# Full-height operands for the small products of a streaming encoder step: zero-padded planes for the remainder of k, and 128 rows and columns for the sample's products and transposes

## The chip, the cores and the metric

One core of one Trainium2 chip runs the whole kernel in one launch. The time is device microseconds of one execution, and the kernel before is given as the median of 3 runs. The trace shows one more, profiled execution. TensorE is called PE, its weight loads PEld, VectorE DVE, ScalarE ACT, GpSimd POOL and the queue that issues the DMAs SP.

## The reference, cut to what matters

The function is one step of a one-layer encoder on two inputs at once: a prompt of 512 rows and a sample of 32 rows with a cache of 512 earlier positions. D is 1024, and everything is f32.

```
h = rms_norm(x);  q, k, v, xb, gb, qc = split(h @ w_in)
# A: differential attention, 8 heads, two 64-wide q/k maps a head, 128-wide values
logits[m] = q_m . k_m / 8 + bias      (m = 0, 1; masked by blocks of 64 positions)
w = softmax(logits[0]) - lam * softmax(logits[1]);  a = rms_norm(w @ v)
# B: a gated linear recurrence over a width-4 convolution of xb
# C: cross attention of qc (4 heads x 256) into 256 memory rows
x += (gate_a * a@Wa + gate_b * b@Wb + gate_c * c@Wc) @ w_out
x += (silu(g) * u) @ w_ffn_out;       y = rms_norm(x)
```

The sample does the same with the cached keys and values in front of its own 32, and with its own cached memory rows. Keys, values, recurrent states and the memory's keys and values are outputs too.

## The kernel before, in words

Activations lie transposed, with features on the 128 partitions and the 544 = 512 + 32 positions in the free dimension. Every large product is made from split operands: an f32 value is held as a high part rounded to fp32r and a low part, the remainder, and a product is high·high + high·low + low·high, each a one-pass fp32r matmul. `gemm` (line 413) does this per 128 output features in two halves of 272 columns into one of two accumulators in PSUM (`acc`). Four further PSUM banks (`side`) serve everything small. Weights come in 1 MB chunks and are split by ACT (`wh`) and DVE (`wl`).

The order of instructions on each engine is fixed when the kernel is built. The class `Flow` (line 48) plays main generators and helper generators against each other by estimated costs: a helper that says `yield t` goes on when the planner's clock reaches t, and `fl.take`/`fl.give` hand out buffers. `MM` (line 307) charges a matmul by its columns alone, whatever its row count. On the chip each engine then runs its list in that order and waits on semaphores.

Stages: the memory's products and the input norm; then "attn" (pairs p = 0..3 of heads, lines 1101 to 1109): the q, k and v products of two heads on the main line, with everything else of the pair slipped in between; then "lru"; then "cross"; then the output product and the FFN. What the change touches:

- `k_evac` (line 869) makes of each head's k a tile `ka` [128, 2, 512]: per map m, the 64 rows of that map's high part in their own half and again in the other half. The remainder goes to `kl` [128, 512], each map in its own 64 rows. `qa` [128, 2, 544] has, per map, the high part of q in the map's rows and the remainder in the others.
- `unit` (line 980), 32 of them, one per head and block of 128 queries, makes the logits of two maps. Per map it issues two products over N = 256, 256, 384 or 512 keys: one over 128 rows (`ka`, which gives high·high + low·high) and one over the map's 64 rows (`kl`, high·low). DVE then adds the bias and takes the minimum (line 1000), ACT makes the exponential, DVE merges the maps, PE transposes (`ident,e`), ACT or DVE copies, and PE multiplies with v (`vn,wt`).
- `natural` (line 856) transposes v: four 128×128 blocks and the sample's 32 columns.
- `sample` (line 916), 4 of them: the sample's attention over 544 keys for two heads. Weights `es` [128, 544] are combined by products with `cm` (four blocks of 128 columns and one of 32), copied to `wts`, and multiplied with the cached v (`vc`) and the new v (`vn`, 32 rows).
- `cross_sample` (line 1391), 4 of them: the sample's cross attention, with 32 columns of q as stationary operand, and a transpose of [32, 256].
- `row_norm` (line 534): sums of squares per position by products with a column of ones, in blocks of 128 positions and a last one of 32, a reciprocal root on DVE, and products with the identity that spread it over the partitions.
- `MB` (line 788): parts of the later tile `m`, lent to the attention stage. `mb done` is the event after which `gate_a` (line 1114) may write the first gates into `m`.

Of the kernel before, what the change touches and what calls it, by code (L numbers as in the profile page):

```python
# [9 lines left out]
F32 = mybir.dt.float32  # L10
# [179 lines left out]
def hybrid_step(ctx: ExitStack, tc, io):  # L190
# [29 lines left out]
    def slot_tile(pool, shape, dt, tag):  # L220
        return pool.tile(shape, dt, name=tag, tag=tag, bufs=NB[tag])
# [312 lines left out]
    def row_norm(pool, sqs, n, rb, ev, late=None):  # L534


        blocks = [(i, min(P, n - i * P)) for i in range((n + P - 1) // P)]
        full = n // P
        v = tu(pool, [P, len(blocks)], F32, "rs")
        if full < len(blocks):  # L540
            nc.vector.memset(v[:, full:], 1.0)

        banks = len(blocks) if len(sqs) > 1 else 1
        yield from fl.take(*["side"] * banks)
        pss = [side_tile() for _ in range(banks)]
        for a, sq in enumerate(sqs):
            if a:
                yield from fl.get(late)
            for i, r in blocks:
                MM(pss[i % banks][:r, i:i + 1], sq[:, i * P:i * P + r], ones_d, a == 0, a == len(sqs) - 1)  # L550
        yield fl.now + 100
        for i, r in blocks if banks > 1 else [(slice(0, full), P)] + blocks[full:]:
            ps = pss[i % banks if banks > 1 else 0]
            cols = i if isinstance(i, slice) else slice(i, i + 1)
            t = VS(v[:r, cols], ps[:r, cols], EPS, None, OP.add)
# [8 lines left out]
        for i, r in blocks:  # L564
            o = (i % 4) * P
            MM(pss[i // 4][:, o:o + r], y[:r, i:i + 1].to_broadcast([r, P]), ident[:r, :r], True, True)
        if rb is None:
            S[ev, "bank"] = pss[0]
            fl.set(ev, fl.now + 100)
            return  # L570
        yield fl.now + 100
        for q in range(nb):
            m_ = min(512, n - q * 512)
            t = COPY(rb[:, q * 512:q * 512 + m_], pss[q][:, :m_])
            fl.give("side", t)
        fl.set(ev, t)
# [210 lines left out]

    MB = {"kcT": (0, 1024), "bs": (2048, T), "qpad": (2048 + 2 * T, 256)}

# [66 lines left out]
    def natural(src, dst, j):  # L856
        yield from fl.take("side", "side")
        ps, p2 = side_tile(), side_tile()
        for t in range(4):
            TR(ps[:, t * P:(t + 1) * P], src[:, t * P:(t + 1) * P])  # L860
        TR(p2[:TS, :P], src[:, TP:])
        yield fl.now + 100
        t1 = COPY(dst[:, 0:4, j * P:(j + 1) * P], ps.rearrange("p (t d) -> p t d", t=4))
        t2 = VC(dst[:TS, 4, j * P:(j + 1) * P], p2[:TS, :P])
        fl.give("side", t1)
        fl.give("side", t2)
        yield max(t1, t2)

    def k_evac(at, p, j):
        def go(acc):  # L870
            yield from fl.take("t1")
            kf = t1_tile()
            t = COPY(b2(kf), acc[:, :, :HT])
            give_acc(t)
            S["kf", p, j] = kf
            yield t
# [8 lines left out]
            S["k", p, j] = (ka, kl)  # L885
            yield t
            for m_ in range(2):
                r = slice(m_ * 64, m_ * 64 + 64)
                t = LO(kl[r], kf[r, :TP], ka[r, m_])
            fl.set(("k", p, j), t)  # L890
            for i in range(4):
                fl.spawn(member("attn", unit(at, p, j, i)))
        return lambda acc: member("attn", go(acc))

    def v_evac(at, p, j):
        def go(acc):
# [4 lines left out]
            if j == 0:  # L901
                yield from fl.take("vn")
                S["vn", p] = slot_tile(at, [P, 5, 256], F32, "vn")
            yield t
# [11 lines left out]
    def sample(at, p):  # L916
# [18 lines left out]
        fl.give("bs", t)  # L935
        if p == 3:
            fl.set("mb done", t)
        yield t + 100
# [7 lines left out]
        ps = side_tile()  # L946
        wts_ = slot_tile(at, [P, 5, 64], F32, "wts")
# [6 lines left out]
        t = VC(wts_[:TS, 4], ps[:TS, 256:320])  # L954
        fl.give("side", t)
# [3 lines left out]
        for j in range(2):  # L959
            for t in range(5):  # L960
                r = P if t < 4 else TS
# [18 lines left out]
    def unit(at, p, j, i):  # L980
# [9 lines left out]
        for m_ in range(2):  # L990
            r = slice(m_ * 64, m_ * 64 + 64)
# [18 lines left out]
        if S["units", p, j] == 4:  # L1010
            for tg in ("qa", "ka", "kl"):
                fl.give(tg)
            fl.give("b4", t)
        yield t + 100
# [39 lines left out]
    def finalize(at, p):  # L1054
        if S["left", p]:
            return
        fl.give("vn")
        mn, sm, ss, cc = S["st", p]
        r0 = tu(at, [P, 8], F32, "r0")
# [331 lines left out]
    def cross_sample(cr, h):  # L1391
# [7 lines left out]
        yield from fl.take("ce", "side")  # L1399
        sx = side_tile()[:TS, :NMEM]  # L1400
        for j in range(2):
            MM(sx, S["qsm"][:, 2 * h + j], ckT[:, j], j == 0, j == 1)
        fl.give("ck")
        e = slot_tile(cr, [P, NMEM], F32, "ce")[:TS]
        yield fl.now + 100
# [6 lines left out]
        pts = tu(cr, [P, 2, TS], F32, "pts")  # L1412
        yield fl.now + 100
        t = VC(pts, ps[:, :2 * TS].rearrange("p (t q) -> p t q", t=2))
        fl.give("side", t)
# [6 lines left out]
        fl.give("cv")  # L1422
        yield fl.now + 100
        pov = po[:, :2 * TS].rearrange("p (n q) -> p n q", n=2)
# [214 lines left out]
    def main():  # L1639
# [23 lines left out]
        with tc.tile_pool(name="attn", bufs=1, reuse_waits="tile") as at:  # L1663
            declare(kcT=2, vc=1, bs=2, b4=3, qpad=2, qa=2, ka=2, kl=2, vn=2, es=1, cm=1,
                    wts=1, e=4, wt=2, on=2, ajunk=1)
# [24 lines left out]
        with tc.tile_pool(name="cross", bufs=1, reuse_waits="tile") as cr:  # L1690
            S["cr"] = cr
            declare(mraw=2, mh=2, ml=2, cq=4, ce=4, pth=1, ptl=1, ck=1, cv=1)
            S["qsm"] = tl(cr, [P, 8, TS], F32, "qsm")
            ch = tl(actp, [P, KD, T], F32R, "ah")
# [102 lines left out]
```

## Time and profile before

| what | value |
|---|---|
| median of 3 runs (lowest, highest) | 1266.03 us (1261.21, 1267.73) |
| profiled execution, device time | 1265.88 us |
| its span | 1264.0 us |
| mean granted clock of TensorE | 0.990 |
| PE busy, PEld busy | 1249.7 us (99%), 1214.8 us (96%) |
| DVE, ACT, POOL busy | 677.3 us (54%), 466.7 us (37%), 28.6 us (2%) |

Busy time of PE counts each matmul from its start to its modelled end, and neighbours overlap. So how fast PE goes is read from the starts of its matmuls in the timeline, not from its busy share. A shape such as 64\*128 64x256 is rows × columns of the stationary operand and then rows × columns of the moving one. An f32 product that isn't fp32r appears as two records.

### The profile page before, as it was taken

Reading aid. Unit: us, or ns where it says so; the run is one execution under the profiler, and the core shown is the slowest. Engines: PE = TensorE matmul, PEld = TensorE weight load, DVE = VectorE, ACT = ScalarE, POOL = GpSimd, SP = SyncE. Lnnn points to the kernel's source line nnn. Section 1 sums busy time; section 2 is a strip of 40 time slices with the busy share of each in tenths; the row PEclk is TensorE's granted clock in tenths of the full one; section 3 lists DMA queues with packets and bytes.
Section 4 is the critical chain, followed back from the end, with each engine's and each line's share of the span. In section 5 each row is a group of like instructions: output and inputs, shape, how many; then the busy total and the mean of one; then the engine's idle time right before and its main releaser. Section 6 shows DMA issues by size and latency. Waiting matters only on the chain.

```text
span 1264.0 us, 22469 instructions
## 1 busy us (share of the span) xinstructions
PE 1249.7 (99%) x9620; PEld 1214.8 (96%) x9620; DVE 677.3 (54%) x1338; ACT 466.7 (37%) x781; POOL 28.6 (2%) x88
## 2 busy tenths in 40 slices
PE   8999999999999999999999999999999999999996
PEld 8998989898999999999999999999999999999996
DVE  6875767676526787644545334554344343344235
ACT  6635343434325556732323322343222231222122
POOL 0002000000000111000000000000000000000001
PEclk9999899999999999999999999999999999999998
DMA  7772323231131322233143233222221222212212
GB/s 265 243 239 86 132 85 132 86 102 52 67 109 68 109 76 90 87 118 121 64 139 100 102 132 101 76 92 77 91 101 68 101 79 89 101 68 101 85 51 71
DMA packets 36835, 131.19 MB, mean 104 GB/s; under 512 B 4184, under 2 KB 15832, under 8 KB 25088
## 3 DMA queue, kind: packets, MB, share of 16 engines
q1 hardware_dynamic: 36736, 129.76, 30.2%
q8 instruction: 75, 1.23, 0.4%
q14 instruction: 24, 0.20, 0.0%
HBM read 118.81 MB, written 13.68 MB: 105 GB/s over the span
## 4 chain that ended last, share of the span: by engine, by line
PE 96%; DVE 2%; DMA 1%; ACT 0%; issue 0%; SPq 0%; DVEq 0%; ACTq 0%
PE acc L308 84%; PE side L308 10%; PE side L315 2%; DMA mk_d<-mkf 1%; DMA raw<-in_w_mem_kv 0%; DVE wl L249 0%; DVE x L258 0%; DVE xT L258 0%; DVE rst L249 0%; DVE al L249 0%; ACT wh L236 0%; DVE m L249 0%; ACT m L236 0%; SPq L300 0%; DVE hl L249 0%
## 5 line engine op out<-in xcount | busy, mean ns | idle before, releaser
L308 PE MATMUL acc<-hh,wh 128*128 128x272 f32 x1856 | 389.7, 291 | 0.0
L308 PE MATMUL acc<-hl,wh 128*128 128x272 f32 x1856 | 388.0, 290 | 0.0
L236 ACT ACTIVATE wh<-raw 128x1024 fp32r<-128x1024 f32 (+1 forms) x179 | 187.6, 1049 | 356.5 <-PE acc L308 333.6
L308 PEld LDWEIGHTS acc<-hh,wh 128*128 128x128 f32 x1856 | 292.5, 189 | 2.0 <-issue 0.9
L308 PEld LDWEIGHTS acc<-hl,wh 128*128 128x128 f32 x1856 | 292.0, 189 | 0.4 <-issue 0.2
L249 DVE TENSOR_TENSOR wl<-raw,wh 128x1024 fp32r<-128x1024 f32 (+1 forms) x180 | 217.2, 1208 | 103.8 <-PE acc L308 78.9
L308 PE MATMUL acc<-hh,wl 128*128 128x272 f32 x1856 | 258.3, 289 | 0.0
L308 PEld LDWEIGHTS acc<-hh,wl 128*128 128x128 f32 x1856 | 241.9, 189 | 1.2 <-issue 0.6
L249 DVE TENSOR_TENSOR t<-acc,rb 128x544 f32<-128x544 f32 x44 | 31.9, 725 | 151.3 <-PE acc L308 151.2
L308 PE MATMUL acc<-ah,wh 128*128 128x272 f32 (+2 forms) x480 | 101.4, 288 | 0.0
L308 PE MATMUL acc<-al,wh 128*128 128x272 f32 (+2 forms) x480 | 101.3, 289 | 0.0
L308 PE MATMUL acc<-bl,wh 128*128 128x272 f32 x384 | 79.6, 288 | 0.0
L308 PE MATMUL acc<-bh,wh 128*128 128x272 f32 x384 | 79.5, 288 | 0.0
L249 DVE TENSOR_TENSOR x<-acc,x 128x544 f32<-128x544 f32 (+2 forms) x35 | 23.6, 675 | 103.2 <-PE acc L308 103.2
L308 PEld LDWEIGHTS acc<-ah,wh 128*128 128x128 f32 x480 | 76.4, 188 | 0.0
L308 PEld LDWEIGHTS acc<-al,wh 128*128 128x128 f32 x480 | 76.2, 188 | 0.0
L308 PE MATMUL acc<-ah,wl 128*128 128x272 f32 (+2 forms) x480 | 66.0, 288 | 0.0
L308 PEld LDWEIGHTS acc<-ah,wl 128*128 128x128 f32 x480 | 62.4, 188 | 0.0
L308 PEld LDWEIGHTS acc<-bh,wh 128*128 128x128 f32 x384 | 60.4, 188 | 0.0
L308 PEld LDWEIGHTS acc<-bl,wh 128*128 128x128 f32 x384 | 60.1, 188 | 0.0
L308 PE MATMUL acc<-bh,wl 128*128 128x272 f32 x384 | 52.8, 289 | 0.0
L308 PEld LDWEIGHTS acc<-bh,wl 128*128 128x128 f32 x384 | 49.8, 188 | 0.0
(248 smaller groups left out, 1325.9 us busy)
## 6 DMA issues: line engine op xcount, KB each, us to landing
raw<-in_w_in SPq DMA_DIRECT2D x24, 1024.0 KB, 4.9
raw<-in_w_ffn_in SPq DMA_DIRECT2D x22, 1024.0 KB, 4.9
raw<-in_w_gate SPq DMA_DIRECT2D x12, 1024.0 KB, 5.0
raw<-in_w_ffn_out SPq DMA_DIRECT2D x8, 1024.0 KB, 4.9
raw<-in_w_mem_kv SPq DMA_DIRECT2D x7, 1024.0 KB, 5.7
raw<-in_w_proj_a SPq DMA_DIRECT2D x4, 1024.0 KB, 5.0
raw<-in_w_proj_b SPq DMA_DIRECT2D x4, 1024.0 KB, 4.9
raw<-in_w_proj_c SPq DMA_DIRECT2D x4, 1024.0 KB, 4.9
```

Source lines behind the costliest of these rows:

```text
L236: nc.scalar.activation(out, in_, func, scale=scale, bias=bias, accum_out=accum_out)
L249: nc.vector.tensor_tensor(out, a, b, o)
L308: nc.tensor.matmul(out, lhsT=lhsT, rhs=rhs, start=start, stop=stop)
L315: nc.tensor.transpose(out, in_, ident[:n, :n])
```

## The change

Products over fewer than 128 rows or onto fewer than 128 columns get operands of 128.

- The remainder of k becomes [128, 2, 512] per head, one plane per map, with the other map's 64 rows zero. Two such tiles are made and zeroed once when the attention stage opens, and handed round by a list. The `kl` product then runs over all 128 rows.
- The sample's part of `vn` and `wts` gets zero rows below the 32 (zeroed once), and the products run over 128 rows.
- The last block of `es`, of v, and of the squares is the last 128 positions rather than the last 32, and the results are read from rows 96 to 127.
- The sample's queries of the cross attention are the last 128 columns, in a tile with two buffers, and its softmax and transposes run over 128 rows. The softmax's small statistics are columns of one tile.
- `es` moves into the lent part of `m`, so `mb done` comes after the products that read it.

```diff
@@ row_norm
-        blocks = [(i, min(P, n - i * P)) for i in range((n + P - 1) // P)]
+        blocks = [(i, min(i * P, n - P)) for i in range((n + P - 1) // P)]
-            for i, r in blocks:
-                MM(pss[i % banks][:r, i:i + 1], sq[:, i * P:i * P + r], ones_d, a == 0, a == len(sqs) - 1)
+            for i, o in blocks:
+                MM(pss[i % banks][:, i:i + 1], sq[:, o:o + P], ones_d, a == 0, a == len(sqs) - 1)
-            MM(pss[i // 4][:, o:o + r], y[:r, i:i + 1].to_broadcast([r, P]), ident[:r, :r], True, True)
+            c, r = (i % 4) * P, min(P, n - i * P)
+            MM(pss[i // 4][:, c:c + r], y[:, i:i + 1].to_broadcast([P, P]), ident[:, P - r:], True, True)
@@ natural
-        TR(p2[:TS, :P], src[:, TP:])
+        TR(p2[:, :P], src[:, T - P:])
@@ k_evac
-            kl = slot_tile(at, [P, TP], F32R, "kl")
+            i_kl = S["kl free"].pop(0)
+            kl = S["kl", i_kl]
-                t = LO(kl[r], kf[r, :TP], ka[r, m_])
+                t = LO(kl[r, m_], kf[r, :TP], ka[r, m_])
@@ unit
-            MM(s_[:, :N], qa[r, m_, i * P:(i + 1) * P], kl[r, :N], False, True)
+            MM(s_[:, :N], qa[:, m_, i * P:(i + 1) * P], kl[:, m_, :N], False, True)
@@ sample
-        es = slot_tile(at, [P, T], F32, "es")
+        es = mb("es", 0)
-        if p == 3:
-            fl.set("mb done", t)
...
-        MM(ps[:TS, 256:320], es[:, PAST:], cm, True, True)
+        MM(ps[:, 256:320], es[:, T - P:], cm, True, True)
         fl.give("es")
+        if p == 3:
+            fl.set("mb done")
...
-                lw = vc[:, t, j * P:(j + 1) * P] if t < 4 else vn[:TS, 4, j * P:(j + 1) * P]
-                MM(ps[:, j * TS:(j + 1) * TS], lw, wts_[:r, t, j * TS:(j + 1) * TS], t == 0, t == 4)
+                lw = vc[:, t, j * P:(j + 1) * P] if t < 4 else vn[:, 4, j * P:(j + 1) * P]
+                MM(ps[:, j * TS:(j + 1) * TS], lw, wts_[:, t, j * TS:(j + 1) * TS], t == 0, t == 4)
@@ soft_rows
-        st = tu(S["cr"], [P, 3], F32, "cst")[:s_.shape[0]]
+        i_st = S["cst n"] = S.get("cst n", -1) + 1
+        st = S["cst"][:, 3 * i_st:3 * i_st + 3]
@@ c_evac
+            if j == 0:
+                yield from fl.take("qs")
+                S["qs", h] = slot_tile(cr, [P, 2, P], F32, "qs")
+                fl.set(("qs", h))
+            yield from fl.get(("qs", h))
-            t = VC(S["qsm"][:, 2 * h + j], acc[:, 1, HT - TS:HT])
+            t = VC(S["qs", h][:, j], acc[:, 1, HT - P:HT])
@@ cross_sample
-            MM(sx, S["qsm"][:, 2 * h + j], ckT[:, j], j == 0, j == 1)
+            MM(sx, S["qs", h][:, j], ckT[:, j], j == 0, j == 1)
-            TR(ps[:, t * TS:(t + 1) * TS], e[:, t * P:(t + 1) * P])
+            TR(ps[:, t * P:(t + 1) * P], e[:, t * P:(t + 1) * P])
@@ main, where the attention stage opens
+            S["wts"] = tl(at, [P, 5, 64], F32, "wts")
+            S["vn free"] = [tu(at, [P, 5, 256], F32, "vnz") for _ in range(2)]
+            for z in [S["wts"]] + S["vn free"]:
+                nc.vector.memset(z[:, 4], 0.0)
+            S["kl free"] = [0, 1]
+            for q in S["kl free"]:
+                S["kl", q] = tu(at, [P, 2, TP], F32R, "klz")
+                for m_ in range(2):
+                    nc.vector.memset(f(S["kl", q][64 - m_ * 64:128 - m_ * 64, m_]), 0.0)
```

## Rows read from the trace of the kernel before

**Rows 1.** Busy time by stage: us, busy and count by engine, clock, DMA.
```profile
core 0: us, PE busy (x) PEld busy (x) DVE busy (x) ACT busy (x) POOL busy (x), PEclk, DMA share, GB/s
80.00:346.00 266.00, 266.00 (x1845) 238.59 (x1844) 178.90 (x554) 106.44 (x255) 7.96 (x24) 0.98 0.31 104
346.00:540.00 194.00, 194.00 (x1546) 194.00 (x1546) 128.52 (x178) 107.56 (x169) 15.53 (x54) 1.00 0.26 88
```
**Rows 2.** The page's chain that ended last, by engine.
```profile
PE 96%; DVE 2%; DMA 1%; ACT 0%; issue 0%; SPq 0%; DVEq 0%; ACTq 0%
```
**Rows 3.** Waits of the weight loads in the attention stage: total us, times, longest.
```profile
PEld side L308 <- issue: 11.0, 51, 0.3
...
PEld side L308 <- DVE on L265: 0.2, 1, 0.2
...
PEld side L308 <- DVE e L258: 0.2, 1, 0.2
```
**Rows 4.** Timeline of PE, logits of 256, 384 and 512 keys: start, us.
```profile
86.69 0.28 PE L308 MATMUL side<-ka,qa 128*128 128x256 f32 x1
86.90 0.38 PE L308 MATMUL side<-kl,qa 64*128 64x256 f32 x1
87.21 0.38 PE L308 MATMUL side<-ka,qa 128*128 128x256 f32 x1
...
89.09 0.52 PE L308 MATMUL acc<-hh,wl 128*128 128x272 f32 x2
...
118.33 0.42 PE L308 MATMUL side<-ka,qa 128*128 128x384 f32 x1
...
119.79 0.55 PE L308 MATMUL side<-cm,es 128*128 128x64 f32 x3
...
123.11 0.40 PE L308 MATMUL side<-ka,qa 128*128 128x512 f32 x1
...
124.72 0.41 PE L308 MATMUL side<-wts,vc 128*128 128x32 f32 x2
```
**Rows 5.** Timeline of PE, 128-row products in the cross attention's logits.
```profile
563.22 0.40 PE L308 MATMUL side<-mh,cq 128*128 128x256 f32 x2
...
565.00 0.42 PE L308 MATMUL acc<-bl,wh 128*128 128x272 f32 x2
```
**Rows 6.** Groups by form on PE: count, busy, mean ns.
```profile
L308 PE MATMUL side<-kl,qa 64*128 64x256 f32 x32 | 12.2, 381 | 0.0
L308 PE MATMUL side<-kl,qa 64*128 64x512 f32 x16 | 7.9, 495 | 0.0
L308 PE MATMUL side<-kl,qa 64*128 64x384 f32 x16 | 7.0, 438 | 0.0
```
**Rows 7.** Timeline of PE, the sample's small products.
```profile
107.75 0.71 PE L315 MATMUL side<-ident,t 128*128 128x128 f32 x5
108.29 0.83 PE L308 MATMUL side<-vn,wt 128*128 128x128 f32 x6
...
322.35 0.97 PE L308 MATMUL side<-wts,vc 128*128 128x32 f32 x8
323.25 0.40 PE L308 MATMUL side<-wts,vn 32*128 32x32 f32 x2
...
324.92 0.52 PE L308 MATMUL acc<-hh,wl 128*128 128x272 f32 x2
...
569.13 0.30 PE L315 MATMUL side<-ident,ce 32*128 32x32 f32 x2
569.36 0.50 PE L308 MATMUL side<-mh,cq 128*128 128x256 f32 x2
569.70 0.28 PE L308 MATMUL side<-ml,cq 128*128 128x256 f32 x1
```
**Rows 8.** Busy time around two falls of the clock, columns as in rows 1.
```profile
119.70:126.50 6.80, 6.80 (x45) 5.48 (x44) 2.83 (x12) 3.92 (x9) 0.00 (x0) 1.00 0.00 0
126.50:133.40 6.90, 6.90 (x32) 6.77 (x32) 4.99 (x14) 1.68 (x5) 0.00 (x0) 0.51 0.59 159
133.40:140.20 6.80, 6.80 (x58) 6.80 (x58) 2.03 (x5) 2.96 (x5) 0.00 (x0) 1.00 0.41 171
...
198.20:201.60 3.40, 3.40 (x18) 3.40 (x17) 2.92 (x19) 0.74 (x1) 0.00 (x0) 0.50 0.78 228
```
**Rows 9.** Timeline of DVE and PE where the attention stage opens.
```profile
67.91 0.27 DVE L800 MEMSET m<- 128x256 f32 x1
69.35 1.22 DVE L249 TENSOR_TENSOR wl<-raw,wh 128x1024 fp32r<-128x1024 f32 x1 [1.17 <-ACT wh L236]
70.61 1.46 DVE L249 TENSOR_TENSOR qa<-acc,qa 64x544 fp32r<-64x544 f32 x2
72.08 0.39 DVE L265 COPY m<-acc 64x32 f32<-64x32 f32 x2
...
74.85 0.41 PE L308 MATMUL acc<-hh,wh 128*128 128x272 f32 x2
```
**Rows 10.** Timeline of ACT and PE around the first gate of the stage.
```profile
314.64 0.70 ACT L236 ACTIVATE m<-acc,bgh 128x544 f32<-128x544 f32 x1
...
319.47 1.23 PE L308 MATMUL side<-cm,es 128*128 128x64 f32 x10
320.63 0.52 PE L308 MATMUL acc<-hh,wl 128*128 128x272 f32 x2
...
327.67 0.60 PE L308 MATMUL acc<-hh,wh 128*128 128x272 f32 x2
```

More of the change, by code (lines that the diff above doesn't have):

```diff
@@ L534, in row_norm @@
     def row_norm(pool, sqs, n, rb, ev, late=None):
-        blocks = [(i, min(P, n - i * P)) for i in range((n + P - 1) // P)]
-        full = n // P
+        blocks = [(i, min(i * P, n - P)) for i in range((n + P - 1) // P)]
         v = tu(pool, [P, len(blocks)], F32, "rs")
-        if full < len(blocks):
-            nc.vector.memset(v[:, full:], 1.0)
         banks = len(blocks) if len(sqs) > 1 else 1
@@ L548, in row_norm @@
                 yield from fl.get(late)
-            for i, r in blocks:
-                MM(pss[i % banks][:r, i:i + 1], sq[:, i * P:i * P + r], ones_d, a == 0, a == len(sqs) - 1)
+            for i, o in blocks:
+                MM(pss[i % banks][:, i:i + 1], sq[:, o:o + P], ones_d, a == 0, a == len(sqs) - 1)
         yield fl.now + 100
[L552 to L555, printed above, removed]
+        for cols in [slice(i, i + 1) for i, _ in blocks] if banks > 1 else [slice(0, len(blocks))]:
+            ps = pss[cols.start % banks if banks > 1 else 0]
+            t = VS(v[:, cols], ps[:, cols], EPS, None, OP.add)
         for _ in pss:
@@ L563, in row_norm @@
         pss = [side_tile() for _ in range(nb)]
-        for i, r in blocks:
-            o = (i % 4) * P
-            MM(pss[i // 4][:, o:o + r], y[:r, i:i + 1].to_broadcast([r, P]), ident[:r, :r], True, True)
+        for i, o in blocks:
+            c, r = (i % 4) * P, min(P, n - i * P)
+            MM(pss[i // 4][:, c:c + r], y[:, i:i + 1].to_broadcast([P, P]), ident[:, P - r:], True, True)
         if rb is None:
@@ L786, in cs_ @@
         return slice(p * 256, (p + 1) * 256)
-    MB = {"kcT": (0, 1024), "bs": (2048, T), "qpad": (2048 + 2 * T, 256)}
+    MB = {"kcT": (0, 1024), "bs": (2048, T), "qpad": (2048 + 2 * T, 256), "es": (2560 + 2 * T, T)}
     def mb(tag, p):
@@ L860, in natural @@
             TR(ps[:, t * P:(t + 1) * P], src[:, t * P:(t + 1) * P])
-        TR(p2[:TS, :P], src[:, TP:])
+        TR(p2[:, :P], src[:, T - P:])
         yield fl.now + 100
         t1 = COPY(dst[:, 0:4, j * P:(j + 1) * P], ps.rearrange("p (t d) -> p t d", t=4))
-        t2 = VC(dst[:TS, 4, j * P:(j + 1) * P], p2[:TS, :P])
+        t2 = VC(dst[:TS, 4, j * P:(j + 1) * P], p2[P - TS:, :P])
         fl.give("side", t1)
@@ L885, in go @@
             S["k", p, j] = (ka, kl)
+            S["i_kl", p, j] = i_kl
             yield t
@@ L902, in go @@
                 yield from fl.take("vn")
-                S["vn", p] = slot_tile(at, [P, 5, 256], F32, "vn")
+                S["vn", p] = S["vn free"].pop(0)
             yield t
@@ L946, in sample @@
         ps = side_tile()
-        wts_ = slot_tile(at, [P, 5, 64], F32, "wts")
+        wts_ = S["wts"]
         for t in range(4):
             MM(ps[:, t * 64:(t + 1) * 64], es[:, t * P:(t + 1) * P], cm, True, True)
-        MM(ps[:TS, 256:320], es[:, PAST:], cm, True, True)
+        MM(ps[:, 256:320], es[:, T - P:], cm, True, True)
         fl.give("es")
+        if p == 3:
+            fl.set("mb done")
         yield fl.now + 100
         VC(wts_[:, 0:4], ps[:, :256].rearrange("p (t d) -> p t d", t=4))
-        t = VC(wts_[:TS, 4], ps[:TS, 256:320])
+        t = VC(wts_[:TS, 4], ps[P - TS:, 256:320])
         fl.give("side", t)
@@ L960, in sample @@
             for t in range(5):
-                r = P if t < 4 else TS
-                lw = vc[:, t, j * P:(j + 1) * P] if t < 4 else vn[:TS, 4, j * P:(j + 1) * P]
-                MM(ps[:, j * TS:(j + 1) * TS], lw, wts_[:r, t, j * TS:(j + 1) * TS], t == 0, t == 4)
+                lw = vc[:, t, j * P:(j + 1) * P] if t < 4 else vn[:, 4, j * P:(j + 1) * P]
+                MM(ps[:, j * TS:(j + 1) * TS], lw, wts_[:, t, j * TS:(j + 1) * TS], t == 0, t == 4)
         fl.give("vc")
@@ L990, in unit @@
         for m_ in range(2):
-            r = slice(m_ * 64, m_ * 64 + 64)
             s_ = side_tile()
             MM(s_[:, :N], qa[:, m_, i * P:(i + 1) * P], ka[:, m_, :N], True, False)
-            MM(s_[:, :N], qa[r, m_, i * P:(i + 1) * P], kl[r, :N], False, True)
+            MM(s_[:, :N], qa[:, m_, i * P:(i + 1) * P], kl[:, m_, :N], False, True)
             sl_.append(s_)
@@ L1012, in unit @@
                 fl.give(tg)
+            S["kl free"].append(S["i_kl", p, j])
             fl.give("b4", t)
@@ L1057, in finalize @@
         fl.give("vn")
+        S["vn free"].append(S["vn", p])
         mn, sm, ss, cc = S["st", p]
@@ L1399, in cross_sample @@
         yield from fl.take("ce", "side")
-        sx = side_tile()[:TS, :NMEM]
+        sx = side_tile()[:, :NMEM]
         for j in range(2):
-            MM(sx, S["qsm"][:, 2 * h + j], ckT[:, j], j == 0, j == 1)
+            MM(sx, S["qs", h][:, j], ckT[:, j], j == 0, j == 1)
+        fl.give("qs")
         fl.give("ck")
-        e = slot_tile(cr, [P, NMEM], F32, "ce")[:TS]
+        e = slot_tile(cr, [P, NMEM], F32, "ce")
         yield fl.now + 100
@@ L1409, in cross_sample @@
         for t in range(2):
-            TR(ps[:, t * TS:(t + 1) * TS], e[:, t * P:(t + 1) * P])
+            TR(ps[:, t * P:(t + 1) * P], e[:, t * P:(t + 1) * P])
         fl.give("ce")
-        pts = tu(cr, [P, 2, TS], F32, "pts")
+        yield from fl.take("pts")
+        pts = slot_tile(cr, [P, 2, TS], F32, "pts")
         yield fl.now + 100
-        t = VC(pts, ps[:, :2 * TS].rearrange("p (t q) -> p t q", t=2))
+        t = VC(pts, ps[:, :2 * P].rearrange("p (t q) -> p t q", t=2)[:, :, P - TS:])
         fl.give("side", t)
@@ L1422, in cross_sample @@
         fl.give("cv")
+        fl.give("pts")
         yield fl.now + 100
@@ L1664, in main @@
             declare(kcT=2, vc=1, bs=2, b4=3, qpad=2, qa=2, ka=2, kl=2, vn=2, es=1, cm=1,
-                    wts=1, e=4, wt=2, on=2, ajunk=1)
+                    e=4, wt=2, on=2, ajunk=1)
             S["oS"] = tl(at, [P, HEADS, TS], F32, "oS")
@@ L1691, in main @@
             S["cr"] = cr
-            declare(mraw=2, mh=2, ml=2, cq=4, ce=4, pth=1, ptl=1, ck=1, cv=1)
-            S["qsm"] = tl(cr, [P, 8, TS], F32, "qsm")
+            declare(mraw=2, mh=2, ml=2, cq=4, ce=4, pth=1, ptl=1, ck=1, cv=1, qs=2, pts=1)
+            S["cst"] = tl(cr, [P, 60], F32, "cst")
             ch = tl(actp, [P, KD, T], F32R, "ah")
```

## The prediction

> **What bounds the kernel now.** I read the page's chain first: PE holds 96% of it [rows 2], so only what shortens PE's list, or makes PE wait, can move the time. Then the stages: in the attention stage (80 to 346 us) PE starts 1845 matmuls in 266 us, 0.144 us each, while in the next one it starts 1546 in 194 us, 0.125 us each [rows 1]. The attention stage holds many small products that should be shorter, not longer, so something there costs time per matmul. It isn't other engines: in that stage the matmuls have no wait on any of them, and the weight loads only single ones of 0.2 us, while 11.0 us of their idle time, 51 times, is "issue", time in which nothing outside held them [rows 3]. The timeline of PE shows what it is. Eight logits products over 256 keys, alternating between 128 rows (`ka`) and 64 rows (`kl`), start at 86.69 us, and the next work starts at 89.09: 0.30 us each [rows 4]. Products of the same 256 columns, also fp32r and also accumulating in a side bank, but all over 128 rows, go from 563.22 to 565.00 us for fifteen (one row shows the first two): 0.119 us each [rows 5]. The reader is to see that it is not the 64-row product alone that is dear: 86.90 to 87.21 (`kl` to `ka`) is 0.31 us, and the next steps repeat it. Each change of the row count, in either direction, costs some 0.18 to 0.2 us.
>
> The Trainium skill has this as a rule: TensorEngine Tiling (Array Packing), section Tiling Modes, says that changing the tiling mode drains the engine. The trace agrees for row counts, with the 0.31 against 0.119 us above. It does not for the column count of a transpose: `natural`'s five transposes, the last onto 32 columns, take 107.75 to 108.29 us, 0.108 us each, with no step in or out [rows 7]. By the rule its 8 transposes would return another 8 × 0.2 to 0.4 us, 1.6 to 3.2 us; by the row nothing, and the sum takes the row.
>
> **The change part by part.** *Logits.* There are 64 `kl` products, 32 over 256 keys, 16 over 384 and 16 over 512 [rows 6], and as many `ka` products beside them. Now: 0.30 us over 256 keys; 118.33 to 119.79 us for four over 384, 0.365 us each; 123.11 to 124.72 for four over 512, 0.40 us each [rows 4]. After: the padded product streams the same number of columns, so its price is that of a 128-row neighbour, 0.119 us at 256. For 384 and 512 no clean row exists; adding 128 and 256 columns at 2.4 GHz gives 0.172 and 0.226, scaling the row by columns gives 0.179 and 0.238; I take 0.175 and 0.232. Gains: 64 × 0.181 = 11.6; 32 × 0.19 = 6.1; 32 × 0.168 = 5.4; together 23.1 us (22.7 to 23.4 by the two ways). The other bound is zero, if the step is not tied to the row count.
>
> *The sample's products.* In `sample` the twenty records of weights times v take 322.35 to 324.92 us, 2.57 us, with 32-row pairs between 128-row ones [rows 7]; at 0.108 us, as the 128-row records of the same view, they take 2.16: 0.4 us, four times, 1.6. The ten `cm` records take 319.47 to 320.63 us, 1.16 [rows 10], against 1.08: 0.1, four times, 0.4 at most; I take 0.3. In `cross_sample` the two 32-row transposes take 0.23 us and the two products behind them 0.34 instead of 0.24 [rows 5, 7]; the two as 128-row ones take 0.22, so 0.1 to 0.2 us a head; 0.6 for four. The queries' products onto 32 columns stream 256 columns either way: 0 to 0.9, I take 0.5. The last block of `row_norm`, three times over 544 or 288 positions, is one 32-row pair each at the step just seen: 0.5. Together 3.5 us, with 1.5 and 5.5 as the ends.
>
> *What is added.* Zeroing on DVE, when the stage opens: a memset of 256 columns took 0.27 us [rows 9]; four of 512 columns at twice that are 2.2 at most, two of 256 are 0.5, one of 64 is under 0.27: up to 2.9 us. They stand in DVE's queue at about 67.9 us, ahead of `wl` and of the remainder of q, which frees an accumulator. DVE has 1.17 us idle there; the rest pushes the end of the copies from 72.47 to at most 74.2 us, and PE claims the next accumulator at 74.85 [rows 9]. By the order of allocation they write where the memory's inputs lay, which no product reads any more by then, so I see nothing for them to wait on. Cost 0; if that cover is gone, up to 2 us.
>
> *Waits that move.* `mb done` comes later: the first gate left its accumulator at 314.64 us and now has to wait for the `cm` products, which end at 320.63. Behind it on ACT stands nothing, since the planner orders it after them. Its accumulator is next claimed when the other one's product is done, at 327.67 [rows 10]: 7 us of cover, cost 0; without cover at most 6 us, once. The two `qs` buffers make a head's queries wait for the sample's logits two heads back; those logits take less than 1 us and each head has four heavy products between, so 0. Wider copies (128 columns for 32, 8 times) and softmax over 128 rows cost DVE and ACT tenths, beside PE.
>
> *What PE meets sooner.* The order on each engine is fixed at build, and the planner charges a product by its columns only. So the list was laid out as if the steps of 0.2 us did not exist, and on the chip every step gave DVE and ACT time that the plan hadn't counted. That cover goes: a unit reaches its transposes up to 0.72 us sooner (four products). The trace has a comparison: in the next stage, made by the same planner with no such steps, DVE is busy 128.5 of 194 us (66%) and ACT 107.6, and PE still starts a matmul every 0.125 us [rows 1]. In the attention stage DVE would be busy 178.9 of about 240 us, 75%, ACT less than there. But four weight loads were just late already, by 0.2 us (two of the four are in [rows 3]). I charge a few such waits of some tenths: 1.5 us, ends 0 and 12.
>
> *The clock.* It fell from 2.4 to 1.2 GHz twice in this stage, 126.5 to 133.4 and 198.2 to 201.6 us [rows 8]: 10.3 us, and up to 5.1 us lost. Before the first fall PE was never idle, but started 45 matmuls in 6.8 us where it does 58 at full pace [rows 8]; it was among 64-row logits and the sample's products. The second pair of heads fell too, the third and fourth with the same work did not, so such a fall isn't certain for this work. With the list denser I expect fewer: 2.5 us gained, ends 5.1 gained and 3.4 lost (two more falls like the shorter one).
>
> **Sum.** 23.1 + 3.5 − 1.5 + 2.5 = 27.6 us. The profiled execution took 1265.88 us, of which the span is 1264.0; the rest stays. 1265.9 − 27.6 = 1238.3; the profiled execution stands 0.15 us below the median, so 1238 for the median too.
>
> **The rivals.** *Half is given back to waits.* The transposes or the products with v reach PE before DVE and ACT have made their operands. Place: `ident,e` and `vn,wt` of each unit. Price: at most the 0.72 us that a unit gains; if half of the 32 units lose it, 11.5 us, and 1250. For it: the late weight loads. Against it: the next stage, and that a unit's own filler, the 0.125-us products of the main line, is untouched.
>
> *The step isn't the row count.* If it came from two products in a row into one bank, the padding would change nothing: 23 us stay, the small products give 0 to 3, and the time is 1264 to 1267. Against it: the fifteen products at 0.119 us also accumulate in one bank by sixes.
>
> *Slower.* DVE's part of a unit's chain sets the pace of the stage: PE stands at each unit for the reductions, the exponential and the merge. It decides from a mean new wait of (23.1 + 3.5) / 32 = 0.83 us a unit on; at 1.2 us, 38 us are lost against 27 gained and the time is about 1278. Against it: PE arrives at most 0.72 us sooner at a unit, so mean waits above that need a plan whose order itself has become worse, which the new buffers (`es`, `qs`, `pts`) could only do by chance.
>
> The same page's rule that small row counts can run beside each other speaks against padding. Here a `kl` product always has a 128-row product on either side and the trace shows no pair beside each other [rows 4], so nothing is given up.
>
> **How the numbers follow.** Forecast 0.79, half given back 0.13, no effect 0.05, slower 0.03. The forecast's own ends: all the better ends give 1265.9 − 23.4 − 5.5 − 5.1 = 1232; small terms at the poor end, waits of 3 us and no help from the clock give 1265.9 − 22.7 − 1.5 + 3 = 1245. The range reaches on to the second case: 1231 to 1251. What can be told from no change is about 0.5%, 6.3 us, so both first cases are faster: 0.92. No effect, 0.05, is the same; 0.03 slower.
>
> **What would show it.** Right: in the attention stage `kl` products read 128\*128 and start 0.12 us after `ka`, the "issue" idle time of the weight loads falls from 11 us to under 3, the stage is some 25 us shorter, and later stages keep their length but for tenths. Wrong: `ka` and `kl` still 0.3 us apart (no effect); new waits of PE on DVE or ACT in the attention stage of over 5 us in total (given back); DVE's memsets followed by a gap of PE at 75 us; or a gap of PE near 327 us, where the gate's accumulator is claimed.

## The result and the profile after

The changed kernel takes **1230.8 us** (median of 4 runs, 1229.9 to 1231.0) where the kernel before took 1266.1 us beside it (1261.2 to 1267.7): a ratio of 0.9726, with a 95% interval from 0.9699 to 0.9753. The forecast was 1238 us, inside 1231 to 1251. The direction and the cause were right. The gain was 35 us where 27.6 were expected, so the time lies at the range's lower edge: the median is 0.2 us under 1231, and the ratio times the 1266.03 us of the forecast gives 1231.3.

The runs of the kernel before spread by 6 us, and the spread goes with the granted clock: of its runs beside the experiments, those at 0.994 took 1261.5 to 1263.7 us and those at 0.989 to 0.990 took 1265.9 to 1267.3. The changed kernel takes 1230.8 at 0.993 to 0.995, so at least 30 of the 35 us don't hang on the clock, and the rest depends on which runs of the kernel before are compared.

The page after: span, busy time by engine, and the chain that ended last, by engine. PE still holds 96% of the chain, as in [rows 2]; its list became shorter, and no other engine took its place.
```profile
span 1229.0 us, 22475 instructions
...
PE 1214.2 (99%) x9620; PEld 1205.5 (98%) x9620; DVE 678.9 (55%) x1340; ACT 466.0 (38%) x781; POOL 28.2 (2%) x88
...
PE 96%; DVE 2%; DMA 1%; ACT 0%; issue 0%; SPq 0%; DVEq 0%; ACTq 0%
```

Busy time of the two stages of [rows 1] in the changed kernel, same columns. The attention stage now runs from 80 to 314 us, 1842 matmuls in 234 us: 0.127 us each, as in the next stage (195 us, 1554, 0.125 us). Before it was 0.144. The weight loads' idle time is nearly gone: 5.3 us, where it was 27.4.
```profile
80.00:314.00 234.00, 234.00 (x1842) 228.70 (x1841) 177.02 (x554) 106.03 (x254) 7.60 (x24) 1.00 0.34 117
314.00:509.00 195.00, 195.00 (x1554) 195.00 (x1553) 128.80 (x179) 108.22 (x170) 15.46 (x54) 1.00 0.26 87
```

The waits of the weight loads in that stage (total us, times, longest) are this one line:
```profile
PEld acc L308 <- issue: 3.8, 16, 0.2
```
In the kernel before, [rows 3] had 11.0 us of "issue", 51 times, at the side banks' loads and single waits for DVE, and the same view had this line beside them, so all its "issue" was 16.6 us:
```profile
PEld acc L308 <- issue: 5.6, 24, 0.2
```
The matmuls have no wait on another engine in the changed stage at all.

The timeline of PE (start in us, duration) at the first logits, against [rows 4], and the first product behind the stage. The `klz` products read 128\*128 and start 0.12 us after `ka`; eight products take 86.90 to 87.85, 0.95 us, where they took 2.40. From its first `ka` to the first `ah,wh` the stage runs from 86.90 to 333.48: 246.58 us.
```profile
86.90 0.28 PE L308 MATMUL side<-ka,qa 128*128 128x256 f32 x1
87.02 0.28 PE L308 MATMUL side<-klz,qa 128*128 128x256 f32 x1
87.14 0.28 PE L308 MATMUL side<-ka,qa 128*128 128x256 f32 x1
...
87.85 0.41 PE L308 MATMUL acc<-hh,wl 128*128 128x272 f32 x2
88.10 0.41 PE L308 MATMUL acc<-hh,wh 128*128 128x272 f32 x2
...
333.48 0.41 PE L308 MATMUL acc<-ah,wh 128*128 128x272 f32 x2
```

In the kernel before the same product behind the stage stood here, so the stage took 364.91 − 86.69 = 278.22 us: 31.64 more.
```profile
364.91 0.41 PE L308 MATMUL acc<-ah,wh 128*128 128x272 f32 x2
```

The groups by form that answer to [rows 6] (count, busy us, mean ns): the same 64 products, on 128 rows, and a mean of 281 ns where it was 381 over 256 keys.
```profile
L308 PE MATMUL side<-klz,qa 128*128 128x256 f32 x32 | 8.2, 281 | 0.0
L308 PE MATMUL side<-klz,qa 128*128 128x512 f32 x16 | 6.3, 393 | 0.0
L308 PE MATMUL side<-klz,qa 128*128 128x384 f32 x16 | 5.4, 337 | 0.0
```

The timeline of PE at the sample's products, against [rows 7, 10]. The ten `cm` records take 1.03 us (288.63 to 289.66; before 1.16), and the twenty of weights times v 2.15 us (291.36 to 293.51; before 2.57, forecast 2.16). The gate's ACT of the accumulator starts at 289.94, after the `cm` products, as foreseen.
```profile
288.63 1.22 PE L308 MATMUL side<-cm,m 128*128 128x64 f32 x10
289.66 0.37 PE L308 MATMUL acc<-hh,wl 128*128 128x272 f32 x1
```
```profile
289.94 0.71 ACT L236 ACTIVATE m<-acc,bgh 128x544 f32<-128x544 f32 x1 [0.81 <-PE side L308]
```
```profile
291.36 0.97 PE L308 MATMUL side<-wts,vc 128*128 128x32 f32 x8
...
292.17 0.39 PE L308 MATMUL side<-wts,vnz 128*128 128x32 f32 x2
...
293.51 0.50 PE L308 MATMUL acc<-hh,wl 128*128 128x272 f32 x2
```

The other covers are read from the opening of the stage, against [rows 9], on DVE and PE. The memsets took 3.0 us (forecast up to 2.9) and pushed the end of the last copy to 74.50 (forecast at most 74.2); PE claims the next accumulator at 75.06 with no gap ahead of it.
```profile
68.08 0.11 DVE L1683 MEMSET wts<- 128x64 f32 x1
68.20 0.54 DVE L1683 MEMSET vnz<- 128x256 f32 x2
68.89 2.37 DVE L1688 MEMSET klz<- 64x512 f32 x4
```
```profile
74.11 0.39 DVE L265 COPY m<-acc 64x32 f32<-64x32 f32 x2
```
```profile
75.06 0.41 PE L308 MATMUL acc<-hh,wh 128*128 128x272 f32 x2
```

Busy time in the only stretch at half clock that the changed kernel's profile has between the first product and the last microseconds (columns as in rows 1). It lies at the start of the kernel; the two falls of [rows 8] inside the attention stage are not there.
```profile
7.30:14.10 6.80, 6.15 (x27) 5.86 (x28) 3.85 (x8) 5.04 (x11) 0.00 (x0) 0.50 1.03 370
```

The weight loads show what a change of the row count does. In the kernel before, the load of `ka` starts at 86.57 us and its matmul at 86.69, so the load runs beside the matmul ahead of it. The load of `kl` starts at 86.90, with its own matmul [rows 4]:
```profile
86.57 0.19 PEld L308 LDWEIGHTS side<-ka,qa 128*128 128x128 f32 x1
...
86.90 0.18 PEld L308 LDWEIGHTS side<-kl,qa 64*128 64x128 f32 x1
```
All 128 changes into and out of a `kl` product are like that: the load starts 1 to 3 ns before its matmul. In the changed kernel the loads of `klz` and of the products behind them start 0.10 to 0.24 us ahead, as here:
```profile
282.92 0.19 PEld L308 LDWEIGHTS side<-klz,qa 128*128 128x128 f32 x1
...
283.15 0.39 PE L308 MATMUL side<-klz,qa 128*128 128x512 f32 x1
```
So at a change the load no longer runs beside the matmul ahead. What in the engine holds it back is not shown.

### The profile page after: what moved, and what is told of

Same layout as the page of the kernel before. It is cut to its first block, busy times and chain, and to the rows that moved or that the text cites. A ratio compares the mean times of both kernels' runs of the same rounds, so it can differ in the third digit from the quotient of the medians.

```text
span 1229.0 us, 22475 instructions
## 1 busy us (share of the span) xinstructions
PE 1214.2 (99%) x9620; PEld 1205.5 (98%) x9620; DVE 678.9 (55%) x1340; ACT 466.0 (38%) x781; POOL 28.2 (2%) x88
## 4 chain that ended last, share of the span: by engine, by line
PE 96%; DVE 2%; DMA 1%; ACT 0%; issue 0%; SPq 0%; DVEq 0%; ACTq 0%
PE acc L308 86%; PE side L308 8%; PE side L315 2%; DMA mk_d<-mkf 1%; DMA raw<-in_w_mem_kv 0%; DVE x L258 0%; DVE wl L249 0%; DVE xT L258 0%; DVE rst L249 0%; DVE al L249 0%; ACT wh L236 0%; DVE m L249 0%; ACT m L236 0%; SPq L300 0%; DVE hl L249 0%
```

## The experiments

The theory was that PE pays for each change of a product's row count, so that the time returns to a kernel in proportion to the row changes left in it. Rivals were that other edits carry the gain, that part of the gain is hidden by waits, and that columns count as rows do. Seven kernels are the changed kernel with one edit, and one is the kernel before with the planes alone. Times are medians, and ratios are to the kernel before, run beside them.

### The logits alone, and all but the logits

The first keeps only the `kl` planes (with their buffers and the zeroing) and has all other small products on 32 rows and columns, as before. The second puts the `kl` product alone back over 64 rows:
```
-            MM(s_[:, :N], qa[:, m_, i * P:(i + 1) * P], kl[:, m_, :N], False, True)
+            r = slice(m_ * 64, m_ * 64 + 64)
+            MM(s_[:, :N], qa[r, m_, i * P:(i + 1) * P], kl[r, m_, :N], False, True)
```


> Only the zero-padded planes of the remainder of k; every other small product has its 32 rows or columns again. Theory (each change of the row count costs a step of about 0.2 us, and the gain is the sum of such steps): of the 35 us, the logits and the products just behind them hold 24 and the clock up to 4.6, the sample, the cross attention and the norms 6 to 7; so 1236 us, 1234 to 1241 (the upper end if the clock falls once or twice again). Rival (the small products' steps matter little, the remainder of the gain is the clock): 1231 to 1233.

> The changed kernel with one line put back: the product with the remainder of k runs over the map's 64 rows again (the planes and their zeroing stay). Theory (a step at each change of row count): the logits take 43 us again instead of 21.6, the products behind them 2 more, and the clock falls in the attention stage may come back with 0 to 4.6 us: 1255 to 1260 us. Rival (the logits were on PE's path only in part and the gain is the clock's and the small products'): under 1250.

The planes alone took 1238.4 us (1237.7 to 1239.2), ratio 0.980 (0.9784 to 0.9816); all but the planes took 1255.6 (1253.9 to 1256.1), ratio 0.9938 (0.9919 to 0.9956). Both lie in the theory's range and outside the rival's. The planes are worth 1255.6 − 1230.8 = 24.8 us, and the stage's length says the same: 271.27 us in the second kernel less 246.58 is 24.7.

The timeline of PE in the second kernel (64-row logits, the rest as changed) shows where that lies. Eight products take 85.35 to 87.75, 2.40 us as before; and the product behind them is affected too: two `hh,wl` take 87.75 to 88.10, 0.35 us, where behind the 128-row product above they take 0.25.
```profile
85.35 0.28 PE L308 MATMUL side<-ka,qa 128*128 128x256 f32 x1
85.56 0.38 PE L308 MATMUL side<-klz,qa 64*128 64x256 f32 x1
85.87 0.38 PE L308 MATMUL side<-ka,qa 128*128 128x256 f32 x1
...
87.75 0.52 PE L308 MATMUL acc<-hh,wl 128*128 128x272 f32 x2
88.10 0.41 PE L308 MATMUL acc<-hh,wh 128*128 128x272 f32 x2
```

### Half the changes of row count, at 64 rows

If a price hangs on each change, an order with fewer changes should save part of it without any padding:
```
-        per m_:  MM(... ka ...)  then  MM(... kl[:, m_, :N] ...)   # 128 rows
+        both MM(... ka ...), then both MM(... kl[r, m_, :N] ...)   # r: 64 rows each
```


> As the run before, with 64 rows, but a unit's four products stand in the order ka, ka, kl, kl instead of ka, kl, ka, kl. Theory (the step belongs to the change of the row count): a unit has two changes instead of four, so half of some 24 us comes back: 1243 to 1248 us, and kl to kl is under 0.15 us at 256 keys. If the two 64-row products, which stand on different halves of the rows, run beside each other as the Trainium skill's TensorE: Matmul & The Clock Gate (Part 3) says of different row groups, 1238 to 1243. Rival (a 64-row product is itself slow, 0.31 us wherever it stands): as the run before, 1255 to 1260.

It took 1237.5 us (1237.1 to 1237.9), ratio 0.9793 (0.9778 to 0.9809). That is lower than any of the ranges: there were fewer steps, and a pair cost less than two products. The timeline of PE in this kernel shows two `ka` that take 0.33 us to the first `kl`, then two `kl` that take only 0.31 us to the next `ka`. Eight products take 86.44 to 87.83: 1.39 us, between 2.40 and 0.95.
```profile
86.44 0.40 PE L308 MATMUL side<-ka,qa 128*128 128x256 f32 x2
86.77 0.39 PE L308 MATMUL side<-klz,qa 64*128 64x256 f32 x2
87.08 0.50 PE L308 MATMUL side<-ka,qa 128*128 128x256 f32 x2
87.52 0.39 PE L308 MATMUL side<-klz,qa 64*128 64x256 f32 x2
87.83 0.52 PE L308 MATMUL acc<-hh,wl 128*128 128x272 f32 x2
```
The reason is in the group of these products: each lasts 381 ns, as in [rows 6], but the 32 of them keep PE busy for 6.2 us instead of 12.2, so they lie on top of each other by pairs. All 32 pairs in the trace start 3 or 4 ns apart.
```profile
L308 PE MATMUL side<-klz,qa 64*128 64x256 f32 x32 | 6.2, 381 | 0.0
```
The Trainium skill has this in TensorE: Matmul & The Clock Gate, Part 3, Packing small matmuls: products on different row groups of the array run concurrently. The trace agrees, at 3 to 4 ns. It still doesn't beat the padding: the steps around the pair cost more than the second product saves. Entering it costs 0.09 us (0.21 from `ka` to `kl`, against 0.12), leaving it 0.19 (0.31), and the product behind is late by 0.1, as in the kernel above: 0.38 us a pair, 12.2 for 32 pairs. The 32 products that lie beside another save 16 × 0.120 + 8 × 0.175 + 8 × 0.231 = 5.2. The difference is 7.0 us; the stage is 253.75 − 246.58 = 7.2 us longer, and the medians are 6.7 apart.

Since the pair runs side by side, this kernel alone doesn't exclude that a product over few rows is slow by itself. The trace of the kernel before does: ahead of the input norm's spread four 32-row records stand in a row (`oh,rt`), and the third starts 0.43 us after the second, which has 512 columns (44.85 to 45.27); 128-row records of 512 columns (`acc<-m`) start 0.43 us apart too (112.22 to 112.65). Few rows cost nothing there, where no change stands between.

### The transpose onto 32 columns

The forecast weighed a rule of the Trainium skill (TensorEngine Tiling (Array Packing), Tiling Modes) against a row and took the row. This kernel puts that transpose alone back:
```
-        TR(p2[:, :P], src[:, T - P:])
+        TR(p2[:TS, :P], src[:, TP:])
...      # and the copy that reads it
```


> The changed kernel with the last transpose of v in natural onto 32 columns again, 8 transposes in all. Theory from the trace (a transpose onto 32 columns costs no step): 1230.8 us within 0.6, and 0.109 us into and out of it. Rival (the rule that any change of the tiling mode drains the engine): 1.6 to 3.2 us more, 1232.4 to 1234.

It took 1230.5 us (1230.2 to 1230.9), ratio 0.9738 (0.9722 to 0.9753), and its attention stage 246.56 us against 246.58. The row was right: a transpose onto 32 columns has no step. On PE's timeline the five take 104.85 to 105.39, 0.108 us each, the 32-column one among them.
```profile
104.85 0.71 PE L315 MATMUL side<-ident,t 128*128 128x128 f32 x5
105.39 0.50 PE L308 MATMUL side<-vnz,wt 128*128 128x128 f32 x3
```

### How much cover DVE had

The first rival said that half the gain goes to waits for DVE and ACT. These two kernels give DVE more work in each of the 32 units, ahead of the merge, once or twice, without the planner being told; the values do not change:
```
+        for _ in range(1):        # second kernel: range(2)
+            nc.vector.scalar_tensor_tensor(e[1][:, :nk], e[1][:, :nk], 1.0, e[1][:, :nk], OP.mult, OP.max)
```


> The changed kernel with one more DVE instruction in each of the 32 units, between the exponentials and the merge (the second map's weights times 1, result unchanged), about 0.55 us each and 17.6 us of DVE in all; the planner isn't told of it, so the order is that of the changed kernel. Theory (DVE has cover throughout the attention stage, which is why none of PE's gain went back to waits): under 2 us slower, 1230 to 1233. Rival (the cover was used up by the gain, as the term of 1.5 us and the case of half given back supposed): a third or more of the 17.6 us shows, 1236 or more.

> The same with two such instructions, about 1.1 us a unit and 35 us of DVE, which brings DVE to some 220 of 246 us in the attention stage. Theory: here the cover ends in places, and waits of PE on DVE appear in the attention stage: 1233 to 1245. Rival (DVE is far from mattering at any unit): 1231 to 1233. Second rival (no cover): 17 us or more, 1248 and above.

Once: 1230.7 us (1229.4 to 1231.4), ratio 0.974 (0.9711 to 0.9769), no different from the changed kernel. The group of the added instructions (count, busy us, mean ns, then DVE's idle time before them) shows 15.5 us more work, none of which PE saw:
```profile
L1014 DVE SCALAR_TENSOR_TENSOR e<-e 128x128 f32<-128x128 f32 (+3 forms) x32 | 15.5, 483 | 0.4 <-ACT e L236 0.3
```
Twice: 1236.3 us (1236.0 to 1236.9), ratio 0.9785 (0.9762 to 0.9809): 5.5 us slower than the changed kernel for some 31 us of work. Here the waits of the matmuls (total us, times, longest) name DVE for the first time:
```profile
PE side L315 <- DVE e L258: 3.0, 8, 0.5
```
The attention stage is 6.5 us longer (253.04 against 246.58), and by the starts this stands at the transposes of `e`: 5.7 us of it are thirteen of them that come 0.2 to 0.65 us later, so at most thirteen of the 32 units. So after the change every unit had cover on DVE for one such instruction (0.48 us in the mean), and the tightest ones not for two; the others had more. The rival named the right place (the transposes of `e`) and the wrong point: the 0.72 us that a unit gains did not use up the cover.

### The norm's last spread product

A small term, and a riddle beside it: the FFN stage became 1.55 us shorter though nothing in it was charged more than 0.3 us. This kernel puts the last spread product ahead of the FFN, alone, back over 32 rows:
```
+            if r == TS and ev == "rb":
+                MM(pss[i // 4][:, c:c + r], y[P - r:, i:i + 1].to_broadcast([r, P]), ident[P - r:, P - r:], True, True)
```


> The changed kernel with one product put back: in the FFN's norm the last spreading product runs over 32 rows again (rows 96 to 127), two records out of 9620. In the FFN the gemm after it held 125.96 ns per product before and 125.56 after the change, over 2995 products. Theory (this pace is set by the small product that stands last before the long run of equal products and is then kept): pace 125.96 again, from the norm to the last product 1.2 us more on top of 0.3 us for the step itself, so 1232.3 us, 1231.9 to 1232.7. Rival (the pace came from something else that the change moved, such as addresses): 125.56 stays, 0.3 us for the step, 1231.1 us.

It took 1232.3 us (1231.0 to 1233.8), ratio 0.9747 (0.9734 to 0.976). By the times this lies at the edge of what they can tell; by the trace it is plain: the FFN stage (from the norm's first sum of squares to the last 288-column `ah,wh`) took 397.26 us, the length of before (397.28), against 395.73 in the changed kernel. Only some 0.3 us of that is the product itself. The rest is the pace of the heavy products, read from windows of 376 us in that stage (columns as in rows 1) of the kernel before, the changed one and this one, in this order: 2986, 2996 and 2987 matmuls, with PE never idle and the clock at its full level.
```profile
858.00:1234.00 376.00, 376.00 (x2986) 376.00 (x2986) 147.99 (x175) 98.77 (x113) 0.00 (x0) 1.00 0.25 84
```
```profile
824.50:1200.50 376.00, 376.00 (x2996) 376.00 (x2996) 147.94 (x175) 99.64 (x114) 0.00 (x0) 1.00 0.25 85
```
```profile
827.30:1203.30 376.00, 376.00 (x2987) 376.00 (x2986) 147.11 (x174) 98.62 (x113) 0.00 (x0) 1.00 0.25 84
```
From start to start a product takes 125.96 or 125.56 ns, over some 3000 products in a row. Which of the two it is was set by one small product ahead of the run: the edit of two records brought the slower pace back. The other traces agree: the planes alone, which also have the 32-row product there, took 397.28 us for the stage, and the six other kernels with the 128-row one 395.73. What in the engine keeps the pace is open.

### The sample's products alone

The last one puts the sample's last block of weights back onto 32 columns and its product with v back over 32 rows:
```
-        MM(ps[:, 256:320], es[:, T - P:], cm, True, True)
+        MM(ps[:TS, 256:320], es[:, PAST:], cm, True, True)
...      # and the copy that reads it
+                r = P if t < 4 else TS
+                lw = vc[:, t, j * P:(j + 1) * P] if t < 4 else vn[:TS, 4, j * P:(j + 1) * P]
+                MM(ps[:, j * TS:(j + 1) * TS], lw, wts_[:r, t, j * TS:(j + 1) * TS], t == 0, t == 4)
```


> The changed kernel with the sample's attention alone put back: its last block of weights onto 32 columns and its product with the new values over 32 rows, four pairs of heads. Theory (steps at the changes of row count, 0.4 to 0.6 us a pair, which also lengthen the product behind them): 2 to 2.5 us from these, and the clock falls of the attention stage come back in some executions, with up to 1.7 us each: 1232.8 to 1235. Rival (the sample's products cost what the forecast said, 1.9 us, and the clock has nothing to do with them): 1232.5 to 1233 with the same granted clock as the changed kernel, 0.993 to 0.995.

It took 1234.9 us (1232.9 to 1235.2), ratio 0.9768 (0.9754 to 0.9781). On its timeline of PE the last two blocks take until 295.43 from 292.85, 2.58 us as in [rows 7], with the 32-row pair between.
```profile
292.85 0.97 PE L308 MATMUL side<-wts,vc 128*128 128x32 f32 x8
293.75 0.40 PE L308 MATMUL side<-wts,vnz 32*128 32x32 f32 x2
...
295.43 0.52 PE L308 MATMUL acc<-hh,wl 128*128 128x272 f32 x2
```
Its profiled execution, at a granted clock of 0.995, took 1232.9 us, and its attention stage was 249.01 us: 2.4 us more than in the changed kernel, which is the term itself. The other three executions, at 0.993 and 0.994, took 1.8 to 2.3 us more. The question was whether the 32-row products bring the falls of the clock back. In its profile there is none in the attention stage; where the clock fell in the other three is not recorded. So the median lies in the theory's range, the term of 2.4 us is shown, and what the executions took beyond it is not explained.

## Why the prediction was right, and where its sizes were off

The terms, from starts in the profiled executions (span 1264.0 to 1229.0, 35.0 us):

| term | forecast, us | measured, us | from |
|---|---|---|---|
| logits | 23.1 | 24.7 | stage, 271.27 − 246.58 |
| sample's products | 1.9 | 2.4 | stage, 249.01 − 246.58 |
| cross attention | 1.1 | 1.8 | first `bh,wh` to last `mh,cq`, 135.68 to 133.93 |
| last blocks of the norms | 0.5 | 0.9 | 0.3 at each of the three spreads |
| waits | −1.5 | 0 | waits, none of PE |
| clock in the attention stage | 2.5 | 4.5 | what is left of 31.64 |
| pace in the FFN | not seen | 1.2 | stage, 397.28 to 395.73, less 0.3 |
| sum | 27.6 | 35.5 | |

The sum is 0.5 us above the spans' difference. Most of that lies ahead of the attention stage, which begins 0.2 us later than before although the norm ahead of it is 0.3 shorter; the half-clock stretch at the kernel's start lasted 6.8 us in this execution and 3.4 in that of the kernel before.

**The step between row counts: right, and shown.** The rows of the 128-row cross attention gave the price of a padded product correctly: 0.120 us over 256 keys, 0.175 over 384 and 0.231 over 512, where 0.119, 0.175 and 0.232 were taken. Summed over the starts behind all 128 `ka` and `kl` records, that part is 21.8 us. The forecast had 23.1 for it, 1.3 too much, above all because it gave all 128 products their clean price (20.6 us) where they took 21.6: a `ka` behind an f32 product starts its neighbour some 0.09 us late. The remaining 2.9 us are what the forecast missed: it counted the time from each `ka` and `kl` to the next start, but not that one more product behind a run is late. By the starts of the second kernel and the changed one these are 29 products, 0.1 us each. That 23.1 came so near 24.7 is in part luck, since the two errors offset each other. The rival that the step isn't the row count falls with the second kernel.

**The waits: 1.5 us charged, none came.** The covers named held: no wait of PE in the stage, no gap at 75 us, and the gate's accumulator, which `cm` now frees late, is claimed only at 296.24, 6.3 us after the gate's ACT starts. Adding work to DVE showed that this was no near miss; about 0.5 us in every unit was still free. Only the end of the copies at the stage's opening came later than the bound, 74.50 against 74.2, still ahead of PE's claim at 75.06.

The claim of the accumulator on PE's timeline, against the last line of [rows 10]:
```profile
296.24 0.60 PE L308 MATMUL acc<-hh,wh 128*128 128x272 f32 x2
```

**The small terms: all low, by 0.4 to 0.7 us each.** The step was known from the `kl` rows, but was charged at half price where a product is narrow in columns only. In the cross attention the queries' product onto 32 columns was given 0.5 us for four heads out of 0 to 0.9. Four records of it took 0.98 us before (561.78 to 562.76 on that timeline) and take 0.68 now. Inside the run the records start 0.216 us apart before and 0.215 now, so the 0.3 stands at the changes on either side: from the heavy product ahead to the third one behind it is 1.54 us before and 1.22 now, and four heads gave 1.3. On PE's timeline in the changed kernel:
```profile
530.51 1.02 PE L308 MATMUL side<-ck,qs 128*128 128x256 f32 x4
531.19 0.59 PE L308 MATMUL side<-mh,cq 128*128 128x256 f32 x2
```
So a change of the column count costs a step at this product and none at a transpose, a difference that the rows taken then did not show. The weight loads have it too: before, at each of the 16 such changes at the `cm` and the queries' products the load starts 1 to 2 ns before its matmul, and at the transposes of v onto 32 columns 0.11 us ahead.

**The clock: the sign was right, the reason is not shown.** Both falls in the stage are gone from the profile, so nearly the whole upper end (5.1 us) came back instead of half. That is luck in part: runs of the kernel before at a clock of 0.994 are 2 to 4 us shorter than the profiled one at 0.990, and beside such runs the gain would have been smaller by that. The forecast put the falls down to a thin list of 64-row logits. That doesn't hold: the kernel with the 64-row logits has no fall in the stage, and the kernel with the planes alone, whose list is denser, has one, in the window below (columns as in rows 1). It costs at most 1.7 us, half its length, with PE busy all the time.
```profile
242.20:245.60 3.40, 3.40 (x17) 3.40 (x17) 1.98 (x6) 0.28 (x1) 0.00 (x0) 0.51 0.52 159
```
The two profiles with a fall there are those of kernels with the sample's 32-row products, but the last experiment has these too and its profile shows none. What starts a fall stays open; one profile per kernel can't tell.

**The signs.** Two of them did not come as written. The "issue" idle time fell to 3.8 us and not under 3: at the side banks it is gone, and what is left stands at the accumulators' loads, 5.6 us before, which the forecast had not counted. And the later stages did not keep their length but for tenths: the cross attention lost 1.8 us and the FFN 1.55.

**What the forecast argued about concurrency** ("nothing is given up" by padding) was right for the order of the kernel before. It was incomplete: grouped by two, the 64-row products do run beside each other, and an order that uses this takes back 18 of the 24.8 us with 64-row products. No kernel run here is faster than the changed one beyond the spread of its runs.

## What to carry to other kernels

Where products of fewer rows alternate with 128-row ones, compare start-to-start times on PE with those of a pure 128-row run of the same columns; if there is a difference, pad the short operand with zeros, and count the product behind as well. The weight loads tell it too: at such a change the load starts with its own matmul instead of ahead of it. If padding isn't possible, put the short products in pairs on different row halves, so that there is one change for two. Before charging a denser list with new waits, look at what the engine beside it has free per unit: here 0.5 us of DVE or more in every unit stayed unused.

## What the runs showed that was not expected

- In the FFN the run of heavy products keeps one of two paces, 125.96 or 125.56 ns, for 376 us and more; the last small product ahead of it decides which, in all ten traces.
- Two products of 64 rows on different halves start 3 to 4 ns apart, so the second adds 3 to 4 ns to the first.
- A change of the row count costs some 0.09 us at the product that changes and 0.1 at the one behind it, in either direction. A 64-row product between 128-row ones has two changes: 0.09 us going in, 0.19 going out (the 0.1 of the first change and the 0.09 of the second), and 0.1 on the product after that. That is 0.38 us, and 64 × 0.38 = 24.3 of the 24.7 measured. Where the kinds alternate, the last part falls on the next way in, and both steps read 0.31 us, as in [rows 4]. The sample's f32 products pay less, some 0.1 us a change: 0.42 us for the four changes of a pair of heads (2.57 against 2.15 us).
- A change to 32 columns and back costs 0.3 us at the four queries' products (1.54 against 1.22 us with what stands on either side) but none at a transpose (0.108 us with and without).
